# The third product's weights in halves, in every seven-product block of a fused hybrid decoder layer

## The chip, the cores and the metric

One Trainium2 chip, one core. The metric is the device time of one execution in microseconds. A core has a matrix engine (TensorE, PE in the profile, with its weight loads as PEld), a vector engine (DVE), a scalar engine (ACT), GpSimd (POOL) and a queue engine (SP); PE multiplies into banks of PSUM, the others work between PSUM and the on-chip SBUF, and DMA engines move data to and from memory.

## The reference, cut to what matters

One decoder layer on 256 tokens of width 2048, in float32: a half-step SwiGLU network, a token mixer in two groups (a gated linear recurrence and a short gated convolution), a second half-step SwiGLU network, and a final norm.

```python
def swiglu_ffn(x, w_gate, w_up, w_down):          # 2048 -> 5632 -> 2048
    return (jax.nn.silu(x @ w_gate) * (x @ w_up)) @ w_down

x = x + 0.5 * swiglu_ffn(rms_norm(x, ffn1_norm), ffn1_w_gate, ffn1_w_up, ffn1_w_down)
z = rms_norm(x, mix_norm) @ w_in                  # then conv, recurrence, gates
x = x + y @ w_out
x = x + 0.5 * swiglu_ffn(rms_norm(x, ffn2_norm), ffn2_w_gate, ffn2_w_up, ffn2_w_down)
return rms_norm(x, final_norm)
```

The weights of the three matrices of each network, of `w_in` and of `w_out` are some 370 MB in float32, and each is read once.

## The kernel before, in words

**Precision.** Every weight tile is split into a high part, rounded to the matrix engine's reduced float32 type (`F32R`), and a low part, the remainder. A matrix product of a weight tile is then three sums: activations high and low against the weight's high part, activations high against the weight's low part. ACT makes the high part (`hi`, a cast, in two halves of two k-tiles), DVE subtracts it from the raw weights (`lo`). In the trace these are `hi_g_p`, `lo_g_p` and so on, where g, u or d is the gate, up or down matrix, p a weight sum or a weight of one of the seven products, and x a plain weight.

**Seven products.** `seven` computes a block of 256 tokens by 1024 columns over 1024 rows of a weight matrix as two by two blocks with seven multiplications in place of eight. Each of the seven takes 128 tokens, a sum of activation blocks (`sf[i]`) and a sum of weight blocks. A unit of weights is 512 rows by 512 columns, 128 partitions by 2048 numbers, in four k-tiles (`UK`). The seven go in the order 0, 4, 5, 6, 2, 3, 1; the third in that order is `product_of(5, ...)`, and its weight sum is the running sum `w11 + w22`, added in place. For the second one, `product_of(4, ...)`, the sum, the casts and the subtractions are already made in halves of two k-tiles; there `order` tells the planner to keep the subtractions where the program has them. Between the seven, the other two units of the 2048 rows are multiplied plainly by `usual`: `usual(0, b2, 1, ...)` stands ahead of the third product and fills banks e and c. Bank c is free for it only when ACT has copied the second product out (`s5`, traced as `s_g`, `s_u` or `s_d`).

There are 28 such blocks: ten gate and up blocks in each of the two networks, two blocks of the down matrix by `down_pair` in each, and two by `down` in each. Blocks with `fourth` let GpSimd gather a later weight sum by an accumulating DMA into `w11` after the third product.

A product of 128 tokens with one unit is 12 matrix instructions: eight with the high part of the weights, then four with the low part. One undisturbed start follows the last after 0.227 us, so a product takes 2.72 us and a plain unit for 256 tokens 5.44 us.

**Order.** Nothing in `seven` fixes the order of an engine's instructions, except where an instruction is kept in program order. A planner goes over the whole program at compile time, with modelled durations, and takes for each engine what it thinks is ready; the order that comes out is fixed, each engine works through it one after the other, and semaphores make it wait. So the order of the trace is not that of the program. Weight loads are issued by SP into three buffers (`raws`), and a load waits until its buffer has been read by the subtraction of an earlier unit.

**Turning.** The hidden activations are turned by a DMA transpose through a small buffer `pair`: an ACT copy into `pair` (`pair<-z`), the transpose, a copy back, and then a cast `h<-pair` on ACT and a subtraction `h<-pair,h` on DVE. These fall between the products.

**End.** `last(c, t, ps)` finishes each tile of 128 tokens (t is 0, then 1). For the last 512 columns it sums the squares, makes the row factor `r` (`fr` in the trace) in five small steps, scales the 2048 columns in four pieces on ACT and DVE and sends each piece out by a DMA on SP's queue.

Of the kernel before, what the change touches and what calls it, by code (L numbers as in the profile page):

```python
# [14 lines left out]
ALU = mybir.AluOpType  # L15
# [3 lines left out]
D = 2048  # L19
S = 256  # L20
FF = 5632
NT = S // P
# [10 lines left out]
class Engine:  # L33


    pinned = False
# [13 lines left out]
def hybrid_block(ctx: ExitStack, tc: tile.TileContext, a: dict, out: bass.AP):  # L50
    nc = tc.nc
    Engine.pinned = False
    dve, act, pe = (Engine(tc, e) for e in (nc.vector, nc.scalar, nc.tensor))
# [32 lines left out]
    def f32(ap):  # L86
        return ap.bitcast(F32)
# [82 lines left out]
    def splits_of(name):  # L170
        pool, bufs = splits, 2
        if extra:
            turn_of["split"] += 1
            if turn_of["split"] % 3 == 0:
                pool, bufs = extra[0], 1
        hi = pool.tile([P, UK, CW], F32R, tag="hi", name=f"hi_{name}", bufs=bufs)
        lo = pool.tile([P, UK, CW], F32R, tag="lo", name=f"lo_{name}", bufs=bufs)
        return hi, lo, [(hi[:, j, :], lo[:, j, :]) for j in range(UK)]
# [22 lines left out]
    tasks, moving, sides, seen, held = deque(), deque(), [0], set(), {}  # L201
# [194 lines left out]
    def seven(w, rows, cols, sf, xs, name, keep, done, between=None, ready=None, whole=True, order=False, fourth=False, beside=None):  # L396


        a, c, e, d = (bank(f"ps_{name}_{n}") if n != "e" or not beside else None for n in "aced")

        def of(u, n):
            return w[u * UK * P : (u + 1) * UK * P, cols[n] : cols[n] + CW]

        def get(u, n, kept=False):
            return load(of(u, n), f"{name}_{u}{n}", kept=kept)

        def gather(to, u, n):
            nc.gpsimd.dma_start(to, of(u, n).rearrange("(j p) c -> p j c", p=P), accum_op=ALU.add)

        def other(i, u, n):  # L410
            return beside.load(i) if beside else get(u, n) if i % 2 == 0 or two else None

        (r0, r1), two = rows, beside or len(xs) > 1
        u0, u1 = (xs[0][0], xs[-1][0]) if xs else (None, None)
        w11, first = ready or (get(r0, 0, True), None)
        w12 = get(r0, 1, True)
        b2, w22, b3 = other(0, u0, 1), get(r1, 1), other(1, u1, 1)
        a2, w21, a3 = other(2, u0, 0), get(r1, 0), other(3, u1, 0)

        def snap(ps, n, sign=1.0):  # L420
            s = keep(f"{n}_{name}")
            act.activation(s, ps, AF.Copy, scale=sign)
            return s

        def product_of(i, raw, ps, begin=False, end=True, blk=None):
            multiply([(ps, sf[i], begin, end)], blk or parts_of(raw, f"{name}_p{i}"), True)

        def usual(i, raw, n, *targets):

            if beside:  # L430
                beside.multiply(2 * (1 - n) + i, raw)
                return
            blk = parts_of(raw, f"{name}_x{i}{n}")
            multiply([(ps, stationary(xs[i][1], t), b, z) for ps, t, b, z in targets], blk, True)

        product_of(0, w11, a, True, blk=first)
        s1 = None if whole else snap(a, "s1")
        if whole:
            act.copy(d, a)
        hi, lo, blk = splits_of(f"{name}_p4")  # L440
        for i in (0, 2):
            o = slice(i, i + 2)
            dve.tensor_tensor(w11[:, o], w11[:, o], w12[:, o], op=ALU.add)
            act.copy(hi[:, o], w11[:, o])
        for i in (0, 2):
            o = slice(i, i + 2)
            ins = dve.tensor_tensor(lo[:, o], w11[:, o], f32(hi[:, o]), op=ALU.subtract)
            if order:
                tc.keep_in_program_order(ins)
        gather(w12, r1, 1)  # L450
        product_of(4, w11, c, True, blk=blk)
        s5 = snap(c, "s5")
        if between:
            between(0)
        usual(0, b2, 1, (e, 1, True, not two), (c, 0, False, False))
        if between:
            between(1)
        dve.tensor_tensor(w11, w11, w22, op=ALU.add)
        product_of(5, w11, a)
        u2 = snap(a, "u2", -1.0)  # L460
        if fourth:
            gather(w11, r1, 0)
        if between:
            between(2)
        if two:
            usual(1, b3, 1, (e, 1, False, True), (c, 0, False, False))
        product_of(6, w12, a)
        u3 = snap(a, "u3", -1.0)
        done(1, 1, e, [u3, s5])
        product_of(2, w22, c)  # L470
        done(0, 1, c, [u2])
        usual(0, a2, 0, (d, 0, not whole, False), (a, 1, False, False))
        if not fourth:
            dve.tensor_tensor(w11, w11, w21, op=ALU.add)
        product_of(3, w11, a, end=bool(beside) or not two)
        if two:
            usual(1, a3, 0, (a, 1, False, True), (d, 0, False, False))
        done(1, 0, a, [])
        product_of(1, w21, d)
        done(0, 0, d, [] if whole else [s1])  # L480
# [462 lines left out]
    with tc.tile_pool(name="mixer", bufs=1) as mp, tc.tile_pool(name="mixw", bufs=2) as mw:  # L943
# [208 lines left out]
        def row_factor(u):  # L1152
# [4 lines left out]
        order = [  # L1157
            (lru_x, 0, 0), (lru_x, 0, 1), (sc_c, 3, 0), (lru_gate, 1, 0), (sc_x, 4, 0),
            (lru_gate, 1, 1), (sc_c, 3, 1), (sc_x, 4, 1), (sc_b, 2, 0), (sc_b, 2, 1),
        ]  # L1160
# [35 lines left out]
    ov = out.rearrange("(t p) d -> p t d", p=P)  # L1196

    def last(c, t, ps=None):
        if c == 0 and t == 0:
            held["fin"] = bigs.tile([P, D], F32, tag="big", name="fin")  # L1200
            nc.scalar.dma_start(held["fin"], a["final_norm"].partition_broadcast(P))
        fin = held["fin"]
        cs = slice(c * CW, (c + 1) * CW)
        xr = xres[:, t, cs]
        part = fss[:, t, c : c + 1]
        junk = work.tile([P, CW], F32, tag="junk", name=f"junk_f_{c}_{t}", bufs=1)
        if ps is None:
            act.activation(junk, xr, AF.Square, accum_out=part)
        else:
            cut = CW // 2  # L1210
            for o in (slice(0, cut), slice(cut, CW)):
                dve.scalar_tensor_tensor(xr[:, o], ps[:, o], 0.5, xr[:, o], op0=ALU.mult, op1=ALU.add)
            act.activation(junk[:, :cut], xr[:, :cut], AF.Square, accum_out=part)
            rest = fss[:, t, NC_D : NC_D + 1]
            dve.scalar_tensor_tensor(
                pair[:, t, :cut], xr[:, cut:], 1.0, xr[:, cut:], op0=ALU.mult, op1=ALU.mult, accum_out=rest
            )
            dve.scalar_tensor_tensor(held[t], rest, 1.0 / D, held[t], op0=ALU.mult, op1=ALU.add)

        def single(tag):  # L1220
            return work.tile([P, 1], F32, tag=tag, name=f"{tag}_{t}")


        if c < NC_D - 1:
            dve.scalar_tensor_tensor(xr, xr, -0.5, fin[:, cs], op0=ALU.mult, op1=ALU.mult)
            if c == NC_D - 2:
                pre = held[t] = single("pre")
                dve.reduce_sum(pre, fss[:, t, : c + 1], axis=AX.X)
                dve.tensor_scalar(pre, pre, 1.0 / D, EPS, op0=ALU.mult, op1=ALU.add)
                if t == 0:  # L1230
                    lastgain = fin[:, D - CW :]
                    dve.tensor_scalar(lastgain, lastgain, -0.5, None, op0=ALU.mult)
                act.activation(single("root"), pre, AF.Sqrt)
            return
        v, y, q, r = (single(f"f{n}") for n in "vyqr")
        act.activation(y, part, AF.Sqrt, bias=held[t], scale=1.0 / D)
        dve.reciprocal(y, y)
        dve.scalar_tensor_tensor(v, part, 1.0 / D, held[t], op0=ALU.mult, op1=ALU.add)
        dve.scalar_tensor_tensor(q, v, y, y, op0=ALU.mult, op1=ALU.mult)
        dve.scalar_tensor_tensor(r, q, -3.0, y, op0=ALU.add, op1=ALU.mult)  # L1240
        for engine, begin, end in ((act, 0, 256), (dve, 1536, 2048), (act, 256, 768), (dve, 768, 1536)):
            o = slice(begin, end)
            xo = xres[:, t, o]
            if begin == D - CW:
                dve.scalar_tensor_tensor(xo, xo, r, fin[:, o], op0=ALU.mult, op1=ALU.mult)
            elif engine is act:
                act.activation(xo, xo, AF.Copy, scale=r)
            else:
                dve.tensor_scalar(xo, xo, r, None, op0=ALU.mult)
            nc.sync.dma_start(ov[:, t, o], xo)  # L1250

    ffn(2, n2, last)


# [28 lines left out]
```

## Time and profile before

| what | value |
|---|---|
| time, median of 3 runs | 1713.51 us (1710.78 to 1713.71) |
| the profiled execution | 1711.69 us, its span 1709.9 us |
| PE busy | 1687.7 us, 99% of the span, 7447 instructions |
| DVE busy | 1440.0 us, 84%, 1237 instructions |
| ACT busy | 1228.6 us, 72%, 1537 instructions |
| granted clock of TensorE | 0.999 |
| memory read and written | 373.37 MB and 2.10 MB |

In the rows below, `lo_g_p<-raw_g,hi_g_p 128x2048 fp32r<-128x2048 f32 x1` is an instruction that writes tile `lo_g_p` from `raw_g` and `hi_g_p`; buffer numbers are left out, and L43 is a helper's line that all instructions share. A time in square brackets is idle time of the engine just before, with what ended it.

### The profile page before, as it was taken

The numbers are of one execution on the slowest core, as the hardware profiler recorded it, in microseconds if no ns is written. First come the engines' busy times: TensorE is split into PE (matmuls) and PEld (weight loads), VectorE is DVE, ScalarE is ACT, GpSimd is POOL, SyncE is SP. The second block draws the span as 40 slices with busy tenths as digits, with TensorE's granted clock in tenths as the row PEclk, the third lists the DMA queues.
The fourth block names the chain that finished last, engine by engine and source line by source line (L and its number), as shares of the span: only waits on it lengthen the run. The fifth ranks groups of instructions, "written<-read, shape, count | busy, mean of one in ns | idle before, by whom it ended". The sixth has DMA issues, their size and how long they took to land. (4 is left out here: it accounts for less than half of the span.)

```text
span 1709.9 us, 19642 instructions
## 1 busy us (share of the span) xinstructions
PE 1687.7 (99%) x7447; PEld 1388.6 (81%) x7447; DVE 1440.0 (84%) x1237; ACT 1228.6 (72%) x1537; POOL 47.9 (3%) x52
## 2 busy tenths in 40 slices
PE   8999999999999999999999999999999999999998
PEld 7878887888777888888888888888887887888886
DVE  7988988988988878768696679979889989899786
ACT  7867667758757677977777677776567668577764
POOL 1000000000000000000000000000000000000000
PEclk9999999999999999999999999999999999999999
DMA  8778779788788785876667596787788887888873
GB/s 305 224 245 235 222 235 251 211 268 242 207 280 239 232 278 156 251 214 199 206 202 227 179 293 190 237 255 219 248 238 245 244 236 235 245 243 245 252 220 123
DMA packets 271071, 396.68 MB, mean 232 GB/s; under 512 B 86404, under 2 KB 88832, under 8 KB 270848
## 3 DMA queue, kind: packets, MB, share of 16 engines
q1 hardware_dynamic: 253616, 360.75, 65.8%
q0 software_dynamic: 17216, 33.63, 11.7%
q8 instruction: 58, 0.95, 0.2%
q10 hardware_dynamic: 144, 1.05, 0.2%
q14 instruction: 37, 0.30, 0.1%
HBM read 373.37 MB, written 2.10 MB: 220 GB/s over the span
## 5 line engine op out<-in xcount | busy, mean ns | idle before, releaser
L43 ACT CAST hi_u_p<-raw_u 128x1024 fp32r<-128x1024 f32 x140 | 142.1, 1046 | 78.4 <-DVE raw_u L43 26.0
L43 DVE TENSOR_TENSOR lo_g_p<-raw_g,hi_g_p 128x2048 fp32r<-128x2048 f32 (+1 forms) x75 | 152.3, 2033 | 38.8 <-ACT hi_g_p L43 37.7
L43 DVE TENSOR_TENSOR lo_u_p<-raw_u,hi_u_p 128x2048 fp32r<-128x2048 f32 (+1 forms) x80 | 160.5, 2020 | 14.2 <-ACT hi_u_p L43 13.7
L43 PE MATMUL ps_d<-hi_d,h 128*128 128x512 f32 x704 | 167.8, 389 | 0.0
L43 ACT CAST hi_d_p<-raw_d 128x1024 fp32r<-128x1024 f32 x112 | 114.2, 1046 | 59.7 <-DVE raw_d L43 17.2
L43 PEld LDWEIGHTS ps_d<-hi_d,h 128*128 128x128 f32 x704 | 132.1, 188 | 27.6 <-ACT hi_d L43 0.2
L43 PE MATMUL ps_in<-hi_in,xT_nm 128*128 128x512 f32 x640 | 151.9, 390 | 0.0
L43 ACT CAST hi_g_p<-raw_g 128x1024 fp32r<-128x1024 f32 x132 | 133.8, 1044 | 24.4 <-DVE raw_g L43 8.7
L43 PEld LDWEIGHTS ps_in<-hi_in,xT_nm 128*128 128x128 f32 x640 | 119.5, 188 | 24.5
L43 DVE TENSOR_TENSOR lo_d_p<-raw_d,hi_d_p 128x2048 fp32r<-128x2048 f32 (+1 forms) x64 | 128.4, 2020 | 12.4 <-ACT hi_d_p L43 11.0
L43 DVE TENSOR_TENSOR lo_in<-raw_in,hi_in 128x2048 fp32r<-128x2048 f32 x40 | 91.2, 2287 | 45.1 <-ACT hi_in L43 45.1
L43 DVE TENSOR_TENSOR lo_d<-raw_d,hi_d 128x2048 fp32r<-128x2048 f32 x44 | 100.3, 2288 | 33.2 <-ACT hi_d L43 33.1
L43 ACT CAST hi_d<-raw_d 128x1024 fp32r<-128x1024 f32 x88 | 89.2, 1045 | 36.4 <-DMA raw_d<-in_ffn_w_down_dram 20.4
L43 ACT CAST hi_u_x<-raw_u 128x1024 fp32r<-128x1024 f32 x80 | 81.1, 1046 | 44.1 <-PE ps_u_c L43 23.5
L43 ACT CAST hi_g_x<-raw_g 128x1024 fp32r<-128x1024 f32 x80 | 81.2, 1045 | 27.2 <-DMA raw_g<-in_ffn_w_gate_dram 13.2
L43 ACT CAST hi_in<-raw_in 128x1024 fp32r<-128x1024 f32 x80 | 80.7, 1046 | 27.0 <-PE ps_in L43 22.0
L43 DVE TENSOR_TENSOR lo_g_x<-raw_g,hi_g_x 128x2048 fp32r<-128x2048 f32 x40 | 91.4, 2286 | 5.3 <-ACT hi_g_x L43 5.3
L43 DVE TENSOR_TENSOR lo_u_x<-raw_u,hi_u_x 128x2048 fp32r<-128x2048 f32 x40 | 91.4, 2286 | 1.4 <-ACT hi_u_x L43 0.8
L43 PE MATMUL ps_d<-lo_d,h 128*128 128x512 f32 x352 | 87.2, 389 | 0.0
L43 DVE TENSOR_TENSOR raw_u<-raw_u,raw_u 128x1024 f32<-128x1024 f32 (+1 forms) x40 | 69.7, 1755 | 16.7 <-DMA raw_u<-in_ffn_w_up_dram 16.3
L43 PE MATMUL ps_in<-lo_in,xT_nm 128*128 128x512 f32 x320 | 79.0, 389 | 0.0
L43 PEld LDWEIGHTS ps_d<-lo_d,h 128*128 128x128 f32 x352 | 66.1, 188 | 13.7
(405 smaller groups left out, 3683.5 us busy)
## 6 DMA issues: line engine op xcount, KB each, us to landing
raw_d<-in_ffn_w_down_dram SPq DMA_DIRECT2D x88, 1024.0 KB, 5.9
raw_u<-in_ffn_w_up_dram SPq DMA_DIRECT2D x87, 1024.0 KB, 5.5
raw_g<-in_ffn_w_gate_dram SPq DMA_DIRECT2D x86, 1024.0 KB, 6.0
raw_in<-in_w_in_dram SPq DMA_DIRECT2D x40, 1024.0 KB, 5.2
raw_o<-in_w_out_dram SPq DMA_DIRECT2D x16, 1024.0 KB, 5.7
raw_d<-in_ffn_w_down_dram POOLq DMA_DIRECT2D x12, 1024.0 KB, 8.5
raw_g<-in_ffn_w_gate_dram POOLq DMA_DIRECT2D x10, 1024.0 KB, 8.7
raw_u<-in_ffn_w_up_dram POOLq DMA_DIRECT2D x10, 1024.0 KB, 8.7
```

The lines of the kernel that those rows point to most:

```text
L43: ins = getattr(self.engine, name)(*args, **kwargs)
```

## The change

The halves of the second product become a function, `joined`, that is used for the second product as before and for the third as well. For the third product the weight sum was one addition of 128x2048 on DVE, two casts of 128x1024 on ACT, and one subtraction of 128x2048 on DVE; it becomes addition, cast, addition, cast, subtraction, subtraction, all of 128x1024. The third product's subtractions aren't kept in program order.

At the end, the step that makes `v` goes ahead of the reciprocal; the first 256 columns go from ACT to DVE, ACT begins with columns 256 to 768, and DVE follows with 1536 to 2048 and 768 to 1536; and ACT's piece of the last token tile is sent from ACT's own queue in place of SP's.

```diff
-        hi, lo, blk = splits_of(f"{name}_p4")
-        for i in (0, 2):
-            o = slice(i, i + 2)
-            dve.tensor_tensor(w11[:, o], w11[:, o], w12[:, o], op=ALU.add)
-            act.copy(hi[:, o], w11[:, o])
-        for i in (0, 2):
-            o = slice(i, i + 2)
-            ins = dve.tensor_tensor(lo[:, o], w11[:, o], f32(hi[:, o]), op=ALU.subtract)
-            if order:
-                tc.keep_in_program_order(ins)
+        def joined(i, more, pinned=False):
+
+            hi, lo, blk = splits_of(f"{name}_p{i}")
+            halves = [slice(k, k + 2) for k in (0, 2)]
+            for o in halves:
+                dve.tensor_tensor(w11[:, o], w11[:, o], more[:, o], op=ALU.add)
+                act.copy(hi[:, o], w11[:, o])
+            for o in halves:
+                ins = dve.tensor_tensor(lo[:, o], w11[:, o], f32(hi[:, o]), op=ALU.subtract)
+                if pinned:
+                    tc.keep_in_program_order(ins)
+            return blk
+
+        blk = joined(4, w12, order)
         gather(w12, r1, 1)
         product_of(4, w11, c, True, blk=blk)
...
-        dve.tensor_tensor(w11, w11, w22, op=ALU.add)
-        product_of(5, w11, a)
+        blk = joined(5, w22)
+        product_of(5, w11, a, blk=blk)
...
         act.activation(y, part, AF.Sqrt, bias=held[t], scale=1.0 / D)
+        dve.scalar_tensor_tensor(v, part, 1.0 / D, held[t], op0=ALU.mult, op1=ALU.add)
         dve.reciprocal(y, y)
-        dve.scalar_tensor_tensor(v, part, 1.0 / D, held[t], op0=ALU.mult, op1=ALU.add)
...
-        for engine, begin, end in ((act, 0, 256), (dve, 1536, 2048), (act, 256, 768), (dve, 768, 1536)):
+        for engine, begin, end in ((dve, 0, 256), (act, 256, 768), (dve, 1536, 2048), (dve, 768, 1536)):
             o = slice(begin, end)
+            queue = nc.scalar if engine is act and t == NT - 1 else nc.sync
...
-            nc.sync.dma_start(ov[:, t, o], xo)
+            queue.dma_start(ov[:, t, o], xo)
```

## The prediction

> **What bounds the kernel.** The page first: busy times, then the chain.
>
> ```profile
> span 1709.9 us, 19642 instructions
> PE 1687.7 (99%) x7447; PEld 1388.6 (81%) x7447; DVE 1440.0 (84%) x1237; ACT 1228.6 (72%) x1537; POOL 47.9 (3%) x52
> ```
>
> PE is busy 99% of the span. Its instructions are the same before and after. So the change can gain only where PE stands still, and at the end, after PE's last instruction. The chain in order of time gives the undisturbed price of a product, 12 matmuls in 2.72 us, so 0.227 us each:
>
> ```profile
> 1554.55 2.72 PE ps_g_a L43 x12
> 1701.46 0.77 DVE xres L43 x2
> ...
> 1703.31 0.16 DVE fy L43
> 1703.47 0.07 DVE fv L43
> ```
>
> (The last three rows are the end's, for later.) Then the waits, for PE alone, which say what it stood still for (total, times, longest):
>
> ```profile
> PE ps_g_a L43 <- DVE lo_g_p L43: 3.5, 6, 0.6
> ...
> PE ps_u_c L43 <- ACT s_u L43: 1.4, 1, 1.4
> PE ps_u_a L43 <- DVE lo_u_p L43: 1.2, 1, 1.2
> PE ps_g_c L43 <- ACT s_g L43: 0.7, 3, 0.4
> PE ps_d_a L43 <- DVE lo_d_p L43: 0.4, 1, 0.4
> ```
>
> Bank a waiting for a low part of a product's weights (the rows of ps_g_a, ps_u_a and ps_d_a) is 5.1 us in 8 waits. Which product that is, the timeline of one of them tells, a gate block at 414 to 423 us:
>
> ```profile
> 414.29 2.28 DVE L43 TENSOR_TENSOR raw_g<-raw_g,raw_g 128x2048 f32<-128x2048 f32 x1
> 414.85 0.60 ACT L43 ACTIVATE s_g<-ps_g_c 128x512 f32<-128x512 f32 x1
> 415.34 1.05 ACT L43 CAST hi_g_x<-raw_g 128x1024 fp32r<-128x1024 f32 x1
> ...
> 416.28 1.37 ACT L43 COPY pair<-z 128x1024 uint16<-128x1024 uint16 x1
> 416.49 2.29 DVE L43 TENSOR_TENSOR lo_g_x<-raw_g,hi_g_x 128x2048 fp32r<-128x2048 f32 x1
> ...
> 417.51 1.99 ACT L43 CAST hi_g_p<-raw_g 128x1024 fp32r<-128x1024 f32 x2
> ...
> 419.29 1.98 PE L43 MATMUL ps_g_a<-hi_g_p,xs 128*128 128x512 f32 x8
> ...
> 419.53 2.29 DVE L43 TENSOR_TENSOR lo_g_p<-raw_g,hi_g_p 128x2048 fp32r<-128x2048 f32 x1 [0.76 <-ACT hi_g_p L43]
> ...
> 421.88 1.20 PE L43 MATMUL ps_g_a<-lo_g_p,xs 128*128 128x512 f32 x4 [0.62 <-DVE lo_g_p L43]
> ...
> 422.92 1.31 PE L43 MATMUL ps_g_e<-hi_g_x,x 128*128 128x512 f32 x5
> ```
>
> One addition of 128x2048 on `raw_g` is the third product's sum, so this is the product that is changed. Its 12 matmuls run from 419.29 to 422.92, 3.63 us in place of 2.72: 0.91 us lost. The row shows 0.62 of it as idle; the other 0.29 is the overlap of matmuls that the page takes as busy, and a slow restart. Eight waits of 5.1 us with 8 x 0.29 make 7.4 us lost in all. A product whose low part comes late by less than the overlap shows no idle time. One such stands in an up block:
>
> ```profile
> 1504.69 1.75 PE L43 MATMUL ps_u_a<-hi_u_p,xs 128*128 128x512 f32 x7
> ...
> 1507.49 0.85 PE L43 MATMUL ps_u_e<-hi_u_x,x 128*128 128x512 f32 x3
> ```
>
> Eleven matmuls take 2.80 us in place of 2.50: 0.3 lost. That makes 7.7 us in nine products.
>
> **What the halves do in that block.** The low part is late because it is a tail of three whole steps: the whole sum, both casts, the whole subtraction, and the subtraction waits 0.76 us for the second cast. The prices of a whole and of a half, by the sums of the up blocks (mean ns after the comma):
>
> ```profile
> L43 DVE TENSOR_TENSOR raw_u<-raw_u,raw_u 128x2048 f32<-128x2048 f32 x20 | 45.8, 2290 | 16.4 <-DMA raw_u<-in_ffn_w_up_dram 16.3
> ...
> L43 DVE TENSOR_TENSOR raw_u<-raw_u,raw_u 128x1024 f32<-128x1024 f32 x20 | 23.9, 1221 | 0.3
> ```
>
> Two halves cost 2.44 us where a whole cost 2.29, 0.15 more; the subtraction, 2.29 whole in the timeline, I take to split alike. I leave ACT's order as it is (its cast of `hi_g_x` from 415.34, then `pair<-z`, stand in front of the casts in any case), so the first cast still ends near 418.55 and the second at 419.50. DVE adds from 414.29 to 416.7 and does the plain `lo_g_x` until 418.9. Then the first half of the subtraction can go at once, to 420.1, since its cast is done; the second follows to 421.3. PE wants the first half after its eight high matmuls, at 419.29 + 8 x 0.227 = 421.10, and the second two matmuls later, at 421.55. Both are there, and the 0.91 us are gone. Late next on PE is nothing near: the matmuls that follow use `hi_g_x`, cast by 416.4.
>
> The largest loss is another case, in an up block:
>
> ```profile
> 499.87 2.28 DVE L43 TENSOR_TENSOR raw_u<-raw_u,raw_u 128x2048 f32<-128x2048 f32 x1
> 502.07 2.28 DVE L43 TENSOR_TENSOR lo_u_x<-raw_u,hi_u_x 128x2048 fp32r<-128x2048 f32 x1
> 504.27 4.48 DVE L43 TENSOR_TENSOR lo_u_p<-raw_u,hi_u_p 128x2048 fp32r<-128x2048 f32 x2
> ```
> ```profile
> 503.29 2.16 PE L43 MATMUL ps_u_a<-hi_u_p,xs 128*128 128x512 f32 x8
> 506.61 1.20 PE L43 MATMUL ps_u_a<-lo_u_p,xs 128*128 128x512 f32 x4 [1.16 <-DVE lo_u_p L43]
> 507.65 0.63 PE L43 MATMUL ps_u_e<-hi_u_x,x 128*128 128x512 f32 x2
> ```
>
> Here DVE itself is the limit: three instructions without a gap. 4.36 - 2.72 = 1.64 us are lost. In halves, the first subtraction runs from about 504.4 to 505.6, the second to 506.8. PE's last two low matmuls can start at 506.8 where the last two now start near 507.2, so 0.4 to 0.7 us are gained and about 1.0 stays.
>
> **The sum.** 7.7 us of loss less the 1.0 that stays is 6.7 us from the third products. The other 19 show no wait and count nothing. The added DVE time, 28 x 2 x 0.15 = 8.4 us, I cost at nothing: its cover is DVE's idle 269.9 us (1709.9 - 1440.0), and per block it is 0.3 us beside 60 us and more of PE work; without the cover it would cost up to 8.4. ACT's casts are the same in number and size. SP's loads wait for the subtraction that frees a raw buffer; the third product's now ends earlier in the waiting blocks and up to 0.3 us later elsewhere. GpSimd's gather into `w11` waits for the same subtraction and for the casts, with the same shift; neither has a wait of PE behind it in the list above.
>
> **The end.** PE is done by 1701.46, when DVE takes over in the chain; what follows is all on the path.
>
> ```profile
> 1704.68 0.61 DVE L43 TENSOR_SCALAR xres<-xres,fr 128x768 f32<-128x768 f32 x1
> ```
> ```profile
> 1704.54 1.79 SPq L1250 DMA_DIRECT2D out_dram<-xres  x4
> ```
> ```profile
> 1705.00:1706.00 1.00, 0.00 (x0) 0.00 (x0) 0.29 (x1) 0.13 (x1) 0.00 (x0) 1.00 0.52 176
> 1706.00:1707.00 1.00, 0.00 (x0) 0.00 (x0) 0.00 (x0) 0.00 (x0) 0.00 (x0) 0.51 1.05 385
> ```
>
> Moving `fv` ahead of the reciprocal takes its 0.07 us off the chain: it then runs while ACT makes the root. The stages (the last two columns are DMA share and GB/s) show the DMA engines full, 1.05, once 1706 is past: the last megabyte is bound by them, not by the four issues. So what counts is when the first piece starts. It starts at 1704.54, after ACT's piece of 256 columns. On DVE, 768 columns take 0.61 and one column 0.16 (`fy`, in the chain), so 256 take about 0.31, an estimate from these two rows: the first issue comes near 1704.34, 0.2 us earlier. With the 0.07 that is 0.27 us. Sending one piece from ACT's queue brings the last issue (now at about 1705.9) forward; I cost it at nothing between a gain of 0.3 (if issues bound the end) and a loss of 0.4, one issue's time by the SP row (1.79 over 4), if the second queue starts late; full DMA engines are the nearer row.
>
> The Trainium skill, "DMA: Bandwidth & Descriptors", section "Issuing engines are not separate DMA queues", says that transfers from all issuing engines run on the same 16 DMA engines and interleave; by that rule, the trace's 1.05 agrees, the second queue saves issue time alone and the end stays at 0.27.
>
> Sum: 6.7 + 0.27 = 7.0 us. The profiled execution took 1711.69 us, so 1704.7 by its own time; the median of the runs stands 1.8 above it, and from 1713.51 the forecast is 1706.5 us.
>
> **The rivals.** Differences below 0.2%, 3.4 us, are about what a measurement of this kernel can't tell from no change.
>
> *Half the gain.* The planner may put other work between the halves, nothing keeps them together. In the same gate block's second product it did:
>
> ```profile
> 408.44 1.23 DVE L43 TENSOR_TENSOR lo_g_p<-raw_g,hi_g_p 128x1024 fp32r<-128x1024 f32 x1
> 409.59 0.68 DVE L43 TENSOR_TENSOR z<-ps_u_d,z 128x512 f32<-128x512 f32 x1
> 410.34 1.23 DVE L43 TENSOR_TENSOR lo_g_p<-raw_g,hi_g_p 128x1024 fp32r<-128x1024 f32 x1
> ```
>
> With one such instruction of 128x512 (0.68) between the third product's halves, as the turning of the hidden activations has one to place, the second would be ready at 421.9 against 421.55, and 0.35 to 0.5 of the 0.91 stays; in all six gate blocks 2.1 to 3.0. Then 4 us are gained: 1709.5.
>
> *No change.* The order of all engines is made anew, and small waits elsewhere may take back what is gained here. PE's remaining waits, `s_g` and `s_u`, are 2.1 us now; if they and their like grow by 5 or more, the time is 1711 to 1715.
>
> *Slower, by the bank.* PE's longest wait on ACT is an up block's, for the copy that frees bank c:
>
> ```profile
> 102.37 2.00 ACT L43 CAST hi_u_p<-raw_u 128x1024 fp32r<-128x1024 f32 x2 [1.13 <-DVE raw_u L43]
> ...
> 105.22 0.59 ACT L43 ACTIVATE s_u<-ps_u_c 128x512 f32<-128x512 f32 x1
> ```
>
> The third product's casts stand ahead of the copy, and PE waits 1.4 us. With the sum in halves the first cast is ready a half earlier, and the planner can put casts ahead of the copy in more blocks. At about 1.5 us each (wait and restart), the sum turns against the change from the fifth such block on; in ten up blocks more it would be +8, about 1721. Against it: in the gate block above, the copy (414.85) starts before half a sum, begun at 414.29, is done. The same shift may help at 102, by a gain of up to 1.
>
> *Slower, by DVE.* If DVE were the bound, the 8.4 us would show nearly whole and, less the end's 0.3 and a third of the gain, give 1719. Its 84% speak against it; the up block at 500 is such a place, but for 7 us only. The Trainium skill, "VectorE: DVE Perf Modes", section "Rules for kernel authors", says to keep the count of DVE instructions small, since each pays its own flush; by that rule this change is a loss, and the price of 0.15 us a split agrees with a cost per instruction.
>
> **How the numbers follow.** Full gain (4.5 to 9 us): 0.57, prediction 1706.5. Half: 0.18, of which 0.10 above 3.4 us. No change: 0.16. Bank: 0.06. DVE: 0.03. So faster 0.67, same 0.24 (0.16 and 0.08 of the half), slower 0.09. The range: down to 1702.5, with the 1.0 that stays, the 0.3 of issue time and the 1 at 102 all gained too, and about 1.7 off since the three runs before reach from 1710.78 to 1713.71; up to 1713.0, where half and most of no change are in. The likeliest case alone is 1704.5 to 1709.0.
>
> **What would show it.** Right: PE's waits for `lo_g_p` and `lo_u_p` in bank a fall from 4.7 us below 1.5; third products run 2.72 us where they ran 3.63; DVE busy grows by about 8 us; the last tile's first output issue comes 2.8 us after DVE takes over from PE, in place of 3.08 (1704.54 - 1701.46). Wrong: new waits of PE for `s_g`, `s_u`, or another `lo`, or other work between the halves. The forecast fails if the new order costs PE more than the third products lose.

## The result, and the profile after

The changed kernel takes 1709.85 us (median of 19 runs, 1707.63 to 1715.07) against 1713.71 us of the kernel before (19 runs beside them, 1710.78 to 1720.82). The ratio is 0.9977, with a 95% interval of 0.9968 to 0.9986. So 3.9 us are gained where 7.0 were forecast. The profiled executions say the same: 1708.82 us with a span of 1707.0, so 2.9 us less.

The head of the page, then PE's waits (total, times, longest), both of the changed kernel:

```profile
span 1707.0 us, 19692 instructions
PE 1685.6 (99%) x7447; PEld 1390.0 (81%) x7447; DVE 1443.1 (85%) x1295; ACT 1229.6 (72%) x1535; POOL 47.9 (3%) x52
```
```profile
PE ps_g_c L43 <- ACT s_g L43: 4.7, 6, 1.2
...
PE ps_g_c L43 <- DVE lo_g_p L43: 0.8, 2, 0.6
```

Every wait in bank a for a third product's low part is gone: 5.1 us before, none now. The `s_u` wait at 104 us is gone too. In their place stands the wait for `s_g`, ACT's copy that frees bank c in the gate blocks: 0.7 us in 3 waits before, 4.7 in 6 now. A smaller new one is for the second product's low part in bank c.

One gate block shows the exchange. First its timeline before, ACT and PE:

```profile
289.84 1.06 ACT L43 CAST hi_g_x<-raw_g 128x1024 fp32r<-128x1024 f32 x1
290.80 0.59 ACT L43 ACTIVATE s_g<-ps_g_c 128x512 f32<-128x512 f32 x1
...
289.25 1.98 PE L43 MATMUL ps_g_e<-hi_g_x,x 128*128 128x512 f32 x8
291.44 2.11 PE L43 MATMUL ps_g_c<-hi_g_x,x 128*128 128x512 f32 x8 [0.21 <-ACT s_g L43]
...
297.81 1.20 PE L43 MATMUL ps_g_a<-lo_g_p,xs 128*128 128x512 f32 x4 [0.64 <-DVE lo_g_p L43]
298.84 1.99 PE L43 MATMUL ps_g_e<-hi_g_x,x 128*128 128x512 f32 x8
```

The same block after, DVE, ACT and PE:

```profile
283.99 1.22 DVE L43 TENSOR_TENSOR raw_g<-raw_g,raw_g 128x1024 f32<-128x1024 f32 x1
285.12 1.22 DVE L43 TENSOR_TENSOR lo_g_p<-raw_g,hi_g_p 128x1024 fp32r<-128x1024 f32 x1
...
287.78 1.06 ACT L43 CAST hi_g_p<-raw_g 128x1024 fp32r<-128x1024 f32 x1
288.73 1.05 ACT L43 CAST hi_g_x<-raw_g 128x1024 fp32r<-128x1024 f32 x1
289.68 0.60 ACT L43 ACTIVATE s_g<-ps_g_c 128x512 f32<-128x512 f32 x1
...
287.19 1.97 PE L43 MATMUL ps_g_e<-hi_g_x,x 128*128 128x512 f32 x8
290.33 2.11 PE L43 MATMUL ps_g_c<-hi_g_x,x 128*128 128x512 f32 x8 [1.16 <-ACT s_g L43]
...
291.33 2.28 DVE L43 TENSOR_TENSOR lo_g_x<-raw_g,hi_g_x 128x2048 fp32r<-128x2048 f32 x1
293.54 1.22 DVE L43 TENSOR_TENSOR lo_g_p<-raw_g,hi_g_p 128x1024 fp32r<-128x1024 f32 x1
...
295.90 1.07 PE L43 MATMUL ps_g_a<-lo_g_p,xs 128*128 128x512 f32 x4
296.81 1.98 PE L43 MATMUL ps_g_e<-hi_g_x,x 128*128 128x512 f32 x8
```

The third product now runs without a gap. But the first half of its sum (283.99) stands ahead of the second product's last subtraction (285.12), long before it is needed. Its first cast (287.78) is ready that early too, and ACT takes it ahead of the plain cast and the copy. So the copy starts 2.49 us after the plain product (289.68 - 287.19) in place of 1.55 (290.80 - 289.25), and PE waits 1.16 us for bank c in place of 0.21. From one plain product's start to the next the block takes 9.62 us (296.81 - 287.19); before, it took 9.59 (298.84 - 289.25). Nothing is gained here.

In an up block the change does what it says, and more. The one at 500 us, where DVE was the limit:

```profile
499.84 2.36 DVE L43 TENSOR_TENSOR lo_u_p<-raw_u,hi_u_p 128x1024 fp32r<-128x1024 f32 x2
502.11 2.28 DVE L43 TENSOR_TENSOR lo_u_x<-raw_u,hi_u_x 128x2048 fp32r<-128x2048 f32 x1
```
```profile
501.35 1.98 PE L43 MATMUL ps_u_a<-hi_u_p,xs 128*128 128x512 f32 x8
...
504.06 1.98 PE L43 MATMUL ps_u_e<-hi_u_x,x 128*128 128x512 f32 x8
```

The third product takes 2.71 us (504.06 - 501.35) where it took 4.36: its subtractions are now done ahead of the plain one, not after it.

Summed over the trace, this is how late PE's matmuls start. The table adds, from 30 us on, the time beyond 0.227 us of each start that comes more than 0.26 us after the last one; the two columns on the right are experiments told below.

| what PE stands for (us) | before | after | casts behind the copy | gate blocks whole |
|---|---|---|---|---|
| third product, low part, bank a | 7.7 | 0 | 0 | 5.3 |
| plain product, bank c (the copy) | 3.8 | 6.5 | 1.5 | 1.9 |
| second product, gate blocks, bank c | 0.2 | 1.8 | 0.5 | 0.6 |
| down blocks, high parts | 1.3 | 2.6 | 2.9 | 1.5 |
| all, with the rest | 14.8 | 12.8 | 6.5 | 11.0 |

With the smaller delays counted too, before and after are 16.5 and 13.8 us: 2.7 of the 2.9 that the span lost. Each column is one execution, and the smaller rows are not firm: in the one-queue kernel below PE, ACT and DVE have the same orders as in the changed one, and there the second product's row is 0.2 in place of 1.8, and the sum 10.7 in place of 12.8. The copy's row is 6.3 there, against 6.5.

The end, in the timeline of after (DVE takes over at 1698.82), and a stage of the windows (the last two columns are DMA share and GB/s):

```profile
1698.82 0.76 DVE L43 SCALAR_TENSOR_TENSOR xres<-ps_d,xres 128x256 f32<-128x256 f32 x2 [1.34 <-PE ps_d L43]
...
1700.32 0.29 ACT L43 ACTIVATE fy<-fss,pre 128x1 f32<-128x1 f32 x1 [0.54 <-DVE pre L43]
1700.33 0.16 DVE L43 SCALAR_TENSOR_TENSOR fv<-fss,pre 128x1 f32<-128x1 f32 x1
```
```profile
1701.68 1.53 SPq L1255 DMA_DIRECT2D out_dram<-xres  x3
```
```profile
1703.00:1704.00 1.00, 0.00 (x0) 0.00 (x0) 0.00 (x0) 0.00 (x0) 0.00 (x0) 0.72 1.04 387
```

The first output issue comes 2.86 us after DVE takes over (1701.68 - 1698.82), 3.08 before. `fv` runs beside ACT's root, and the 256 columns take 0.35 us on DVE. The DMA engines are full behind it (1.04), as before.

### The profile page after: what moved, and what is told of

Same layout as the page of the kernel before. It is cut to its first block, busy times and chain, and to the rows that moved or that the text cites. A ratio compares the mean times of both kernels' runs of the same rounds, so it can differ in the third digit from the quotient of the medians.

```text
span 1707.0 us, 19692 instructions
## 1 busy us (share of the span) xinstructions
PE 1685.6 (99%) x7447; PEld 1390.0 (81%) x7447; DVE 1443.1 (85%) x1295; ACT 1229.6 (72%) x1535; POOL 47.9 (3%) x52
## 4 chain that ended last, share of the span: by engine, by line
PE 85%; DVE 5%; ACT 5%; DMA 2%; issue 2%; DVEq 0%; SPq 0%; ACTq 0%
PE ps_d L43 13%; PE ps_in L43 12%; PE ps_g_a L43 8%; PE ps_u_a L43 8%; PE ps_u_c L43 6%; PE ps_g_c L43 6%; PE ps_d_a L43 5%; PE ps_o L43 4%; PE ps_g_d L43 4%; PE ps_d_c L43 3%; PE ps_u_d L43 3%; PE ps_u_e L43 3%; PE ps_g L43 3%; PE ps_u L43 3%; PE ps_g_e L43 3%
```

## The experiments

Two theories stood against each other at the start. **The order of ACT**: the half sum is ready early, its cast goes ahead of the copy that frees bank c, and a rule that puts it behind gives the lost microseconds back. **The rival**: ACT has no room, so that any order only moves the wait. Ratios are against the kernel before, run beside each one; its medians there were 1712.49 and 1712.73 us.

**The third product behind the copy.** One constraint is put on the instructions of the third product's `joined`: they are issued after the copy that frees bank c. In the trace this holds for ACT's casts alone. DVE's first half sum keeps its early place (284.06 below), ahead of the copy and of the second product's last subtraction (285.19). The rest of the program is that of the changed kernel, and the planner orders it anew.

```diff
-            act.activation(s, ps, AF.Copy, scale=sign)
+            held["copied"] = act.activation(s, ps, AF.Copy, scale=sign)
...
+        freed = held["copied"]
...
-        blk = joined(5, w22)
+        with tc.issue_after(freed.ins):
+            blk = joined(5, w22)
```

> The changed kernel with one order fixed: the third product's casts stand on ACT behind the copy that frees bank c. Theory (the half sum makes the first cast ready early, the planner sets it ahead of that copy, and PE waits 4.7 us for s_g where it waited 0.7): PE's waits for s_g fall to 1.0 us or less, the third product has no wait, and the time is 3 to 4.5 us below the changed kernel, a ratio to the kernel before of about 0.9955. Rival one (the 56 further DVE instructions cost what is missing): nothing changes, ratio 0.9977. Rival two (the gate block is bound by ACT and DVE together, a wait taken away only moves on): the third product waits for its low part again, 3 us or more, ratio 0.9977.

Measured: 1705.05 us, ratio 0.9954 (0.9940 to 0.9968), span 1701.1. This is the lowest ratio of all. PE's waits:

```profile
PE ps_d_c L43 <- DVE hs L43: 1.2, 3, 0.4
...
PE ps_g_c L43 <- ACT s_g L43: 0.3, 1, 0.3
```

The same gate block, DVE, ACT and PE:

```profile
284.06 1.22 DVE L43 TENSOR_TENSOR raw_g<-raw_g,raw_g 128x1024 f32<-128x1024 f32 x1
...
287.85 1.05 ACT L43 CAST hi_g_x<-raw_g 128x1024 fp32r<-128x1024 f32 x1
288.80 0.59 ACT L43 ACTIVATE s_g<-ps_g_c 128x512 f32<-128x512 f32 x1
289.28 1.04 ACT L43 CAST hi_g_p<-raw_g 128x1024 fp32r<-128x1024 f32 x1
...
287.54 1.97 PE L43 MATMUL ps_g_e<-hi_g_x,x 128*128 128x512 f32 x8
...
295.96 1.98 PE L43 MATMUL ps_g_e<-hi_g_x,x 128*128 128x512 f32 x8
```

One cast changes places with the copy, the third product keeps its halves, and the block takes 8.42 us (295.96 - 287.54) in place of 9.62. The wait for `s_g` falls from 4.7 to 0.3 us, and no low part comes late. So the early half sum by itself costs nothing here; what cost PE its time is the cast that went ahead of the copy. The order of ACT is the cause of the missing gain. How much it is worth is less sure: 3.9 us by the two ratios, whose intervals meet at 0.9968, and 5.9 us by the spans of the two profiled executions. As many DVE instructions run as in the changed kernel, so their number is not what was missing.

**The gate blocks as before.** The other test of the same: the gate blocks' third product stays whole, up and down blocks keep their halves.

```diff
-        blk = joined(5, w22)
+        if name[0] == "g":
+            dve.tensor_tensor(w11, w11, w22, op=ALU.add)
+            blk = None
+        else:
+            blk = joined(5, w22)
```

> The changed kernel, with the gate blocks' third product as in the kernel before (whole sum, whole subtraction); halves in up and down blocks alone. Theory: in the gate blocks the change gains 5 us at the third product and loses 4 to 5 us at bank c, so its gain is from the up and down blocks: waits for lo_g_p 3.5 us and for s_g about 0.7 to 1.5 us as before, none for lo_u_p, lo_d_p and s_u; time within 1.5 us of the changed kernel, ratio 0.997 to 0.9985. Rival (the gate blocks carry the gain): ratio 0.9995 or above.

Measured: 1707.8 us, ratio 0.9974 (0.9966 to 0.9983), span 1705.3.

```profile
PE ps_g_a L43 <- DVE lo_g_p L43: 3.6, 6, 0.7
...
PE ps_g_c L43 <- ACT s_g L43: 0.5, 2, 0.3
```

The six old waits are back, the six new ones nearly gone, and the time is that of the changed kernel within the intervals. So the halves gained nothing on balance in the gate blocks, as far as these times can tell; what was measured came from up and down blocks.

**Halves in casts and subtraction, the sum whole.**

```diff
-        blk = joined(5, w22)
+        dve.tensor_tensor(w11, w11, w22, op=ALU.add)
+        hi, lo, blk = splits_of(f"{name}_p5")
+        halves = [slice(k, k + 2) for k in (0, 2)]
+        for o in halves:
+            act.copy(hi[:, o], w11[:, o])
+        for o in halves:
+            dve.tensor_tensor(lo[:, o], w11[:, o], f32(hi[:, o]), op=ALU.subtract)
```

> The changed kernel with the third product's sum as one addition again; casts and subtractions in halves. Theory: the first cast is not ready early, ACT's order is that of the kernel before, PE's waits for s_g are back at 0.7 us; the low half comes in time in the gate blocks, so their third products stay without a wait; in the up block near 500 us about 1 us stays. Ratio about 0.996. Rival one (DVE instructions): 28 fewer of the 56 give back half of what is missing, ratio 0.997. Rival two (moves on): the wait for the low part is back, ratio 0.9977 or above.

Measured: 1710.53 us, ratio 0.9985 (0.9976 to 0.9994), span 1709.9.

```profile
PE ps_g_c L43 <- ACT s_g L43: 2.4, 5, 0.8
...
PE ps_u_a L43 <- DVE lo_u_p L43: 1.2, 3, 0.4
PE ps_u_c L43 <- ACT s_u L43: 1.1, 1, 1.1
```

A miss, by some 4 us. With the whole sum the up blocks stay late, and the `s_u` wait at 104 us is back: it is the halved sum that clears those. And `s_g` stands at 2.4 us although ACT's order at the copy is that of before: plain cast, then copy. The longest wait:

```profile
1414.60 1.06 ACT L43 CAST hi_g_x<-raw_g 128x1024 fp32r<-128x1024 f32 x1
1415.55 0.60 ACT L43 ACTIVATE s_g<-ps_g_c 128x512 f32<-128x512 f32 x1
...
1416.20 2.11 PE L43 MATMUL ps_g_c<-hi_g_x,x 128*128 128x512 f32 x8 [0.83 <-ACT s_g L43]
```

The copy starts 2.15 us after the plain product (1415.55 - 1413.40). In the kernel before, with the same order in the same block, it was 1.70 (1417.11 - 1415.41), and PE waited 0.36. So here the rival is right in part: with PE no longer held up in bank a, ACT is later against PE at the next copy, and something of the gain moves on. Why that is 2 us here and almost nothing with the third product behind the copy was not settled.

**Halves in sum and casts, the subtraction whole.**

```diff
-        blk = joined(5, w22)
+        hi, lo, blk = splits_of(f"{name}_p5")
+        for o in [slice(k, k + 2) for k in (0, 2)]:
+            dve.tensor_tensor(w11[:, o], w11[:, o], w22[:, o], op=ALU.add)
+            act.copy(hi[:, o], w11[:, o])
+        dve.tensor_tensor(lo, w11, f32(hi), op=ALU.subtract)
```

> The changed kernel with the third product's subtraction as one instruction again; sum and casts in halves. Theory: the early cast is there, so PE waits 4 to 5 us for s_g as in the changed kernel, and the low part comes late again by 3 to 5 us in all: ratio 0.9985 to 1.001. Rival one (DVE instructions): ratio 0.997, better than the changed kernel. Rival two: 0.998.

Measured: 1716.92 us, ratio 1.0023 (1.0014 to 1.0032), span 1714.9: slower than before, and above the 1.001 that was expected at most.

```profile
PE ps_g_c L43 <- ACT s_g L43: 4.5, 6, 1.3
...
PE ps_g_c L43 <- ACT hi_g_p L43: 2.6, 2, 1.9
```

The halved sum alone brings the `s_g` wait, as the theory has it, without a halved subtraction. About half of what came on top is one place at 537 us, where the second product's cast is late by 1.9 us: by the table's rule PE starts 4.6 us late there, against 1.3 in the changed kernel. The same happens in an experiment below, and what it costs is told under the hardware.

**The plain casts behind the copy too.** If ACT has room, the copy can go ahead of the other cast as well. This adds to the first experiment's edit:

```diff
-        def usual(i, raw, n, *targets):
-                blk = parts_of(raw, f"{name}_x{i}{n}")
+        def usual(i, raw, n, *targets, behind=None):
+            with tc.issue_after(behind.ins) if behind else ExitStack():
+                blk = parts_of(raw, f"{name}_x{i}{n}")
...
-            usual(1, b3, 1, (e, 1, False, True), (c, 0, False, False))
+            usual(1, b3, 1, (e, 1, False, True), (c, 0, False, False), behind=freed)
```

> The first experiment's kernel, and the casts of the plain unit that follows the third product also behind the copy that frees bank c. Theory (whatever cast stands ahead of the copy costs PE its time): the 1.2 us that PE still loses at bank c in the gate blocks goes, nothing else changes; ratio 0.9945 to 0.9955. Rival (ACT is short of time in these blocks): the wait shows in the plain unit's high part instead, ratio as in the first experiment or above.

Measured: 1712.46 us, ratio 0.9999 (0.9990 to 1.0008), span 1711.8. The `s_g` wait is gone altogether, and others came:

```profile
PE ps_g_c L43 <- ACT hi_g_p L43: 2.6, 3, 1.7
...
PE ps_d_c L43 <- ACT hs L43: 2.3, 3, 0.9
```

Here the rival is right in the sum, for all that the order had gained is lost again, though not in the place: the plain unit's high part, where it expected the wait, does not stand in the list. By the table's rule PE's late starts are 17.0 us in place of 6.5, and 4.1 of these 10.5 come from one place at 537 us, told under the hardware. What helped was not "the copy first" but one particular cast out of its way.

**The half sum behind the second product's subtractions.** DVE's early half sum also stands between those two; in the changed kernel PE waits 0.8 us for the second of them. This puts the third product's casts behind the copy and its sum behind that subtraction, again on top of the first experiment's edit.

```diff
+            held["low"] = ins
...
+        low4 = held["low"]
...
-        with tc.issue_after(freed.ins):
+        with tc.issue_after(freed.ins), tc.issue_after(low4.ins):
             blk = joined(5, w22)
```

> The first experiment's kernel (casts behind the copy that frees bank c), and the third product's additions on DVE behind the second product's last subtraction. Theory: the waits of bank c for the second product's low part (0.8 us in the changed kernel) are the early half sum squeezed between the second product's two subtractions, so they go to zero here; PE's waits for s_g stay at 1 us or less; ratio 0.994 to 0.996. Rival (the early half sum is needed, it carries the gain): the third product waits again in the gate blocks, 2 us or more, ratio 0.997 or above.

Measured: 1707.1 us, ratio 0.9968 (0.9958 to 0.9978), span 1701.7. The wait is gone, but the first experiment's list had none of it either, and the one-queue kernel told below has none, with DVE's order as in the changed kernel. So the half sum's place is not shown to be its cause. PE's waits in the down blocks for `hs` are 1.7 us in place of 1.2, and the time is no better than with the copy alone; the intervals overlap.

**The end alone**, on the kernel before (the edit is the last part of the change's diff).

> The kernel before with the new end alone. All theories: the waits of PE are those of the kernel before; from DVE's first step after PE to the first output issue 2.87 us in place of 3.08; span 0.1 to 0.3 us shorter; ratio 0.9998 to 1.0000, the interval takes in 1.

Measured: 1713.3 us, ratio 1.0004 (0.9995 to 1.0013). PE's waits are much as before (its late starts by the table's rule are 15.9 us against 14.8). The end shows nothing that can be measured, as its 0.27 us would not. In this build the first issue even comes at 3.16 us (1705.73 - 1702.57), where 2.87 were expected, and the timeline shows where the time goes:

```profile
1704.09 0.16 DVE L43 SCALAR_TENSOR_TENSOR fv<-fss,pre 128x1 f32<-128x1 f32 x1
1704.37 0.29 ACT L43 ACTIVATE fy<-fss,pre 128x1 f32<-128x1 f32 x1 [0.84 <-DVE fv L43]
```

The root starts after `fv`, by the trace released by it, where in the changed kernel `pre` released it and `fv` ran beside it. By its row it reads `fss` and `pre`, not `fv`. Why the wait stands one step later in this build was not tried.

**All output on SP's queue**, with the rest of the changed kernel.

```diff
-            queue = nc.scalar if engine is act and t == NT - 1 else nc.sync
+            queue = nc.sync
```

> The changed kernel with all pieces of the output sent from SP's queue. All theories: PE's waits as in the changed kernel. If the DMA engines bound the end: from DVE's first step after PE to the end of the trace 8.1 to 8.2 us as in the changed kernel. If the issues bound it: 0.2 to 0.3 us more.

Measured: 1707.01 us in a single run, with 4.4 us of waits for `s_g`. From DVE's taking over to the end of the trace it is 8.29 us, with two queues 8.19, before 8.45. So the second queue is worth 0.10 us, as far as single profiled executions can tell: less than the 0.2 to 0.3 of an end bound by issues, though not nothing.

By the traces PE, ACT and DVE run the same instructions in the same order here as in the changed kernel, so it is also a second look at that. The wait for `s_g` came again; the second product's wait for its low part did not, and the span is 1.9 us shorter. Differences of that size between two single executions are not read as effects here.

## Why the prediction was right, and where it was off

**The third products: right, and undersized.** The waits for `lo_g_p` and `lo_u_p` in bank a fell from 4.7 us to none, and the products run in 2.7 us. The 1.0 us that was to stay in the up block at 500 went too: the working kept DVE's order there, but in halves the third product's subtraction went ahead of the plain one. The term is 7.7, not 6.7. Other work did come between the halves, which the prediction had named as a sign of being wrong: in the gate block above the plain subtraction (291.33) runs between the halves (290.20 and 293.54). PE begins with the low part at 295.90 only, so it waits for none of this.

**ACT's order: the step that failed.** "I leave ACT's order as it is" was taken from the trace of a kernel whose sum was ready later. It is the rival "slower, by the bank" that came true, in the gate blocks, and what stood against it was wrong: the half sum "begun at 414.29" was not the place to measure from, for the planner moved that half earlier, to 409.06 in the same block, ahead of the second product's last subtraction. The first experiment shows the rest of the chain: with the cast behind the copy the wait falls from 4.7 to 0.3 us. The price was below the rival's 1.5 us a block: at most 1.2 idle in each of six, and 2.7 us net in the table, since the up block at 104 gained 1.6 by the same shift (the rival had up to 1 there). Beside it the table has 1.6 us more in the second product and 1.3 in the down blocks. The first of these did not come again in the one-queue kernel. The second stays when the copy is put right (2.9 in the first experiment), and its cause was not tested. So the time came out where "half the gain" stood, but not by work between the halves. That it lies no further from 1706.5 is in part luck: gains that were not in the sum, 1.0 at 500 and 1.6 at 104, covered part of a loss that was put at nothing.

**DVE at nothing: right; its price was too high.** DVE's busy time grew by 3.1 us, not 8.4, and in the version with the third product behind the copy by 0.2 (1440.2 us, as many instructions); why these two differ was not worked out. Halves that follow each other overlap: two take 2.36 us together (499.84 above) where the mean durations add up to 2.44 and a whole takes 2.28. So a split costs 0.08 us by these rows, and the 58 further instructions cost less than PE gained. The Trainium skill, "VectorE: DVE Perf Modes", section "Rules for kernel authors", says to keep the count of DVE instructions small. The rows agree that each one more costs something; the time shows that it did not decide here.

**The end: right.** 0.26 us by the profile against 0.27 (8.45 to 8.19), with 0.10 of it from the queue that was costed at nothing. The first issue comes at 2.86 against 2.8; 256 columns take 0.35 us on DVE and not 0.31. The DMA share in the fullest microsecond is 1.04 with two queues and 1.03 with one. The Trainium skill, "DMA: Bandwidth & Descriptors", section "Issuing engines are not separate DMA queues", says that a second issuing engine saves issue time alone. These shares agree.

## What to carry to other kernels

Where a planner makes the order, cutting a step in two changes when its parts are ready, and so what can stand ahead of what on every later engine. A prediction from the old order has to ask, for each part, what it can now overtake. Look for the instruction whose result frees a resource (here the copy of bank c) and ask which early parts may be put ahead of it. If one is, tie that one down and no more: putting the third product's casts behind the copy brought 3.9 us by the ratios, and putting the plain casts behind it too lost all of it again.

## What the runs showed of the hardware

A stall of PE can cost more than its own length. With the plain casts behind the copy, PE stands at 537 and 539 us for a cast, and then the granted clock falls (timeline, then windows, with PEclk third from the end):

```profile
537.19 1.20 PE L43 MATMUL ps_g_c<-hi_g_p,xs 128*128 128x512 f32 x4 [1.69 <-ACT hi_g_p L43]
539.08 1.81 PE L43 MATMUL ps_g_c<-hi_g_p,xs 128*128 128x512 f32 x4 [0.70 <-ACT hi_g_p L43]
540.70 1.91 PE L43 MATMUL ps_g_c<-lo_g_p,xs 128*128 128x512 f32 x4
542.40 0.83 PE L43 MATMUL ps_g_e<-hi_g_x,x 128*128 128x512 f32 x2
```
```profile
535.00:537.00 2.00, 0.49 (x3) 0.07 (x1) 2.00 (x2) 1.91 (x2) 0.00 (x0) 1.00 0.00 0
537.00:539.00 2.00, 1.20 (x4) 0.67 (x4) 1.97 (x4) 2.00 (x4) 1.21 (x1) 1.00 0.58 131
539.00:541.00 2.00, 1.92 (x5) 1.59 (x6) 2.00 (x2) 2.00 (x3) 0.09 (x1) 0.60 0.63 74
541.00:543.00 2.00, 2.00 (x6) 1.43 (x6) 2.00 (x2) 1.61 (x4) 0.00 (x0) 0.54 1.08 195
```

From 540.70 to 542.40 four matmuls start 0.425 us apart in place of 0.227, at about half the clock. In these 4 us that is 1.7 us of PE's time, an estimate from the clock column (2 x 0.40 + 2 x 0.46). No wait in the list shows it: PE counts as busy for 1.92 and 2.00 of each 2 us. The experiment with the subtraction whole has the same fall after the same late cast (0.50 from 541 to 543). The changed kernel stands still at this place too, busy for 2.71 of the 4 us from 537 to 541, and its clock stays at 1.00. Where the limit lies between was not measured. The Trainium skill, "TensorE: Matmul & The Clock Gate", section "Part 1: The HAM clock gate", tells of a clock of one half after a window of about 3.4 us without work; here PE's longest wait was 1.69 us, and it was busy for 1.69 of the 4 us before 539 (0.49 + 1.20). The half clock agrees; the pause that brought it was a shorter one than the page tells of.
